# Layer norms' factors folded into their readers, and expert biases multiplied in float32, in a two-block transformer kernel

## The chip, the cores and the metric

The kernel runs on one core of a Trainium2 chip. The metric is the device time of one execution in microseconds: the median of several runs. Besides these, one execution was recorded by the hardware profiler, and all rows below come from it.

## What is computed

One sequence of 256 rows (T) of 1024 channels (D) goes through two blocks. Only the first is touched by the change:

```python
mix = token_mixer(x, w_in, b_in, sinks, ln_v_g, ln_v_b, w_spatial, b_spatial, w_out, b_out)
h = layer_norm(ALPHA * x + mix, ln1_g, ln1_b)
ffn = routed_experts(h, w_router, b_router, w_gate, b_gate, w_up, b_up, w_down, b_down)
x = layer_norm(ALPHA * h + ffn, ln2_g, ln2_b)
```

The mixer projects x by w_in into attention's q, k, v and into u and g. It runs attention in a window of 128, and beside it a spatial gate: g goes through gelu and a layer norm over groups of 64 channels (factors ln_v_g, ln_v_b), is multiplied along the sequence by a causal 128 x 128 matrix for each of 8 groups, gets b_spatial added, and is multiplied by gelu(u). Both halves together are multiplied by w_out.

The router's logits `h @ w_router + b_router` choose 4 of 32 experts for each row. An expert is `hid = min(x@w_gate+b_gate, 7)*sigmoid(...)*(clip(x@w_up+b_up)+1)`, then `hid @ w_down + b_down`, weighted by a softmax over the four logits. Each of an expert's three matrices is 1024 x 1024 in float32, 4 MiB. The second block (a recurrent mixer, attention and a feed-forward layer) follows.

## The kernel before

**Front** (`front`, lines 195 to 628). The weights of w_in and w_out arrive in pieces of 1 MB in a ring of slots. Each half piece is split into a rounded high part (a cast by ScalarE, line 1324) and a low part (a subtraction, line 1325, by VectorE or POOL as the string FRONT_LOW says); a product is then three fast matmuls (`product`). The order on each engine is the order in which the program lists the instructions; nothing is reordered. `pump` starts the next load and the next casts whenever a product has freed a slot. `after` says which small loads are put into SyncE's queue behind which piece.

POOL computes ALPHA * x at line 339 and adds b_out at line 507. VectorE and POOL normalise one block of g's 128 rows each at lines 499 to 502: subtract the mean, multiply by the inverse deviation, multiply by ln_v_g, add ln_v_b. The spatial product is evicted at lines 523 and 524. The residual then goes through `evict` (line 549, with its statistics at 551), `norm` (559, with ln1_g), `turned` (transposes, copied by ScalarE), `router` (logits, top values; lines 574 and 575) and is scaled by ScalarE (577) and shifted by ln1_b on POOL (578). `split_biases` makes three bf16 parts of b_gate and b_up on rows 0 to 95 of `bgu`, with ScalarE and POOL, between the products by w_out. `warm` issues matmuls without use that keep TensorE busy.

**Experts** (`moe`, from line 699). The chosen rows are found from the logits (lines 709 to 732; `sel` at 726). Each expert gets up to 64 rows. For every two experts `chosen` (744) makes a 0/1 matrix, and `gather` multiplies the normed rows by it, which gives the experts' inputs `xg`, transposed; VectorE (756) and ScalarE (757) evict it. For each expert `gate_up` opens two PSUM banks with the bias, then adds 16 matmuls for the gate and 16 for the up product (64 stationary columns by 512 moving ones; the two halves of the 1024 output channels use the two halves of the array's columns side by side):

```python
self.mm(p[64 * fh:64 * fh + 64, :], self.ohb[:, e:e + 1].to_broadcast([128, CAP]),
        self.bgu[:, q, fh * 512:(fh + 1) * 512], start=True, stop=False)
```

Then come swiglu on VectorE and ScalarE (801 to 806), a transpose of the hidden rows (815, 816), the down product (`y`, evicted at 823), and for two experts together the scatter (`sc`, added into the sum at 772). `start_sum`, at expert 2, writes ALPHA * h plus the weighted b_down into the sum: four matmuls on 32 rows (`sc<-bdn,gT`) and line 965. Expert 15 is finished at once, with a test for overflowing experts behind it.

The experts' weights stream through a ring of nine tiles of 2 MB (`fetch`). SyncE's queue sends for the next tile as soon as TensorE has finished with the oldest one. The first nine tiles are already loaded during the front, in slots that the front gives up one by one.

In the profile all matmuls stand under line 89 and all transposes under line 93, with the names of their tiles: `g`, `u` and `y` are the gate, up and down products, `g<-bgu,ohb` and `u<-bgu,ohb` the biases. A float32 or bf16 matmul of one column half and its neighbour of the other half run side by side.

Of the kernel before, what the change touches and what calls it, by code (L numbers as in the profile page):

```python
# [21 lines left out]
T = 256  # L22
D = 1024
# [16 lines left out]
WARM = 12, 10, 11, 20  # L40
# [31 lines left out]
class Net:  # L72
# [66 lines left out]
    def run(self):  # L139
# [16 lines left out]
        self.bgu = pb.tile([128, 2, D], BF, name="bgu")  # L156
        self.ohb = pb.tile([128, NE], BF, name="ohb")
        nc.gpsimd.memset(self.bgu[96:128], 0.0)
        nc.gpsimd.memset(self.ohb, 0.0)
# [10 lines left out]
        self.top = pb.tile([128, NT, 8], F32, name="top")  # L170
        with ExitStack() as fctx:
            self.front(fctx)
# [28 lines left out]
    def front(self, fctx):  # L201
# [41 lines left out]
        bst = fp.tile([18, 128], F32, name="bst")  # L243
        nc.scalar.dma_start(bst[0:10, :], b_in[0:1280].rearrange("(r c) -> r c", c=128))
        nc.scalar.dma_start(bst[10:18, :], a["ln1_b"].rearrange("o (r c) -> (o r) c", c=128))
# [31 lines left out]
        def after_g():  # L277
            L["bg"] = early(carve(4, 0, (512,)), bcast_rows(b_in[1280:1792], 512))
            L["lnvg"] = early(carve(4, 512, (512,)), bcast_rows(a["ln_v_g"], 512))
            L["lnvb"] = early(carve(4, 1024, (512,)), bcast_rows(a["ln_v_b"], 512))  # L280

        def after_u():
# [5 lines left out]
            L["bout"] = load("bout", [128, D], bcast_rows(a["b_out"], D))  # L288

        def after_wo():  # L290
            L["wr"] = load("wr", [128, KC, NE], a["w_router"][0].rearrange("(k p) e -> p k e", p=128))
            L["br"] = load("br", [128, NE], bcast_rows(a["b_router"], NE))
            L["ln1g"] = load("ln1g", [128, D], bcast_rows(a["ln1_g"], D))
            L["ln1b"] = load("ln1b", [128, D], bcast_rows(a["ln1_b"], D))
            bf = L["bf"] = fp.tile([128, 2 * D], F32, name="bf")
            for s in range(3):
                for q, nme in enumerate(("b_gate", "b_up")):
                    nc.sync.dma_start(bf[32 * s:32 * s + 32, q * D:(q + 1) * D], a[nme][0])

        self.pieces(spec, halves, [slot[f"r{i}"] for i in range(9)])  # L300
        self.after = {0: after_kv, 2: after_q, 4: after_g, 6: after_u, 7: after_wo}
# [13 lines left out]
        p = bank("o", [128, 18])  # L315
# [5 lines left out]
        bqs = fp.tile([128, 18], F32, name="bqs")  # L321
# [16 lines left out]
        for t in range(NT):  # L338
            G.tensor_scalar(self.h[:, t, :], self.x[:, t, :], ALPHA, None, op0=OP.mult)
# [132 lines left out]
        for i in range(3):  # L472
            scores(i)
        pg = [bank("mm", [128, 512]) for _ in range(NT)]
# [30 lines left out]
        r = self.h  # L505
        for t in range(NT):
            G.tensor_tensor(r[:, t, :], r[:, t, :], L["bout"], op=OP.add)
# [6 lines left out]
        for c0 in (0, 2):  # L514
# [8 lines left out]
            V.tensor_tensor(d, p, L["bsb"][:, c0:c0 + 2, None, :].to_broadcast([128, 2, NT, 128]), op=OP.add)  # L523
# [5 lines left out]
        wr, ln1g, ln1b = L["wr"], L["ln1g"], L["ln1b"]  # L529
        lst = [f2.tile([128, 4, 6], F32, tag="lst", name=self.nm("lst")) for _ in range(NT)]  # L530

        def by_experts(rhs, n, E):

            p = bank("s", [128, n])
            for k in range(KC):
                j = k % 4
                self.mm(p[32 * j:32 * j + 32, :], wr[:, k, :], rhs(k), start=k < 4, stop=k >= 4)
            o = f2.tile([128, n], F32, tag=f"le{n}", name=self.nm("le"))
            E(o, p)
            return o  # L540

        cb = fp.tile([128, NE], F32, name="cb")

        bf = L["bf"]
        hT = bf.rearrange("p (k t) -> p k t", k=KC)
# [6 lines left out]

        def norm(t):

            mv = f2.tile([128, 2], F32, tag="lmv", name=self.nm("lmv"))
            V.bn_aggr(mv, lst[t])
            for n in range(2):
                rr = r[:, t, n * 512:(n + 1) * 512]
                V.scalar_tensor_tensor(rr, rr, mv[:, 0:1], ln1g[:, n * 512:(n + 1) * 512],
                                       op0=OP.subtract, op1=OP.mult)  # L560
            return self.rsqrt(f2, mv[:, 1:2], 1, add=1e-5)

        def turned(t):
            for c0 in (0, 4):
                p = bank("s", [128, 4, 128])
                for c in range(4):
                    self.tr(p[:, c, :], r[:, t, (c0 + c) * 128:(c0 + c + 1) * 128])
                S.copy(hT[:, c0:c0 + 4, t * 128:(t + 1) * 128], p)

        def router(t, rs):  # L570
            le = by_experts(lambda k: hT[:, k, t * 128:(t + 1) * 128], 128, S.copy)
            p = bank("s", [128, NE])
# [1485 lines left out]
```

## Time and profile before

| | |
|---|---|
| median of 3 runs | 1548.91 us (1543.96 to 1551.39) |
| the profiled execution | 1553.83 us, of which the span from first to last instruction is 1552.2 us |
| front, to the first gate product | 0 to 124 us |
| experts, to the last down product | 124 to 1044 us |
| second block | 1044 to 1552 us |
| mean granted TensorE clock | 0.966 of 2.4 GHz |
| TensorE matmul busy | 1430.2 us, 92% of the span |
| VectorE, ScalarE, POOL busy | 613.9, 365.4, 179.3 us |
| read from HBM | 488.34 MB |

TensorE's busy time is modelled from starts and so counts some waiting as busy; whether it or the transfers bound a stage must be seen from the stage itself: from the length of a repeated stretch, and from what ended TensorE's idle time.

### The profile page before, as it was taken

What the parts mean: (1) busy time and instruction counts of PE and PEld (TensorE: products, weight loads), DVE (VectorE), ACT (ScalarE), POOL (GpSimd) and SP (SyncE); (2) the same over time, 40 slices, a digit from 0 to 9 for tenths busy, and PEclk for the clock granted to TensorE, in tenths of its full rate; (3) what the DMA queues carried; (4) which work ended last, traced back from release to release, by engine and by line L of the source; (5) the groups of instructions that cost most, each with busy time, mean ns of one, the idle gap of its engine ahead of it and who ended that gap; (6) DMA issues with size and microseconds to landing.
All of it is one profiled execution on the core that took longest, in us unless ns stands there. A gap on an engine that the chain in (4) does not pass through costs nothing. (4 is left out here: it accounts for less than half of the span.)

```text
span 1552.2 us, 19103 instructions
## 1 busy us (share of the span) xinstructions
PE 1430.2 (92%) x7944; PEld 830.2 (53%) x7944; DVE 613.9 (40%) x1087; ACT 365.4 (24%) x607; POOL 179.3 (12%) x155
## 2 busy tenths in 40 slices
PE   8789899999999989999998989897998999999998
PEld 7674333333333333333233233237877777799998
DVE  5882131222122122122124122126597547876664
ACT  4551100010110100100100110113643323365452
POOL 4630000000000011000000000004352223200000
PEclk9999989999999999999999999998988999999999
DMA  9887999999999999999999999983423124765530
GB/s 301 286 332 293 426 409 408 428 427 427 429 427 428 428 425 421 427 429 427 429 426 428 427 427 428 428 334 116 136 89 119 32 86 169 241 220 186 195 136 28
DMA packets 94510, 491.13 MB, mean 316 GB/s; under 512 B 13639, under 2 KB 44039, under 8 KB 67284
## 3 DMA queue, kind: packets, MB, share of 16 engines
q1 hardware_dynamic: 93536, 489.01, 78.2%
q8 instruction: 64, 1.05, 0.3%
q10 hardware_dynamic: 372, 0.66, 0.1%
q0 software_dynamic: 512, 0.20, 0.1%
q14 instruction: 26, 0.21, 0.0%
HBM read 488.34 MB, written 1.51 MB: 316 GB/s over the span
## 5 line engine op out<-in xcount | busy, mean ns | idle before, releaser
L89 PE MATMUL g<-w,xg 128*64 128x512 f32 x1024 | 239.0, 620 | 6.2 <-DMA w<-in_w_gate_dram 6.2
L89 PE MATMUL u<-w,xg 128*64 128x512 f32 x1024 | 227.1, 594 | 13.6 <-DMA w<-in_w_up_dram 13.6
L89 PE MATMUL y<-w,hidT 128*64 128x512 f32 x1024 | 226.9, 595 | 2.9 <-DMA w<-in_w_down_dram 1.7
L89 PEld LDWEIGHTS u<-w,xg 128*64 128x64 f32 x1024 | 70.8, 137 | 159.4 <-issue 132.6
L89 PEld LDWEIGHTS g<-w,xg 128*64 128x64 f32 x1024 | 74.5, 143 | 150.9 <-issue 137.7
L1324 ACT CAST w<-w 128x1024 fp32r<-128x1024 f32 (+1 forms) x116 | 118.7, 1035 | 148.8 <-PE pj L89 62.0
L89 PEld LDWEIGHTS y<-w,hidT 128*64 128x64 f32 x1024 | 70.8, 137 | 152.7 <-issue 144.8
L1325 POOL TENSOR_TENSOR w<-w,w 128x1024 fp32r<-128x1024 f32 (+1 forms) x33 | 79.5, 2413 | 587.8 <-ACT w L1324 582.5
L1325 DVE TENSOR_TENSOR w<-w,w 128x1024 fp32r<-128x1024 f32 x83 | 114.0, 1390 | 83.6 <-ACT w L1324 83.6
L823 ACT COPY y<-y 64x512 f32<-64x512 f32 x64 | 37.1, 579 | 369.8 <-PE y L89 369.4
L801 DVE TENSOR_SCALAR g<-g 128x512 f32<-128x512 f32 x32 | 22.1, 691 | 220.4 <-PE g L89 220.4
L816 DVE COPY hidT<-tr 128x256 f32<-128x256 f32 x32 | 13.6, 425 | 231.7 <-ACT hidT L815 231.7
L804 DVE TENSOR_SCALAR g<-u 128x512 f32<-128x512 f32 x32 | 22.1, 692 | 172.5 <-PE u L89 172.5
L89 PE MATMUL pj<-w,h2p 128*128 128x512 f32 x336 | 84.3, 408 | 0.9 <-DVE w L1325 0.9
L802 ACT ACTIVATE sg<-g 128x512 f32<-128x512 f32 x32 | 20.2, 630 | 244.9 <-DVE g L801 244.9
L89 PEld LDWEIGHTS pj<-w,h2p 128*128 128x128 f32 x336 | 64.2, 195 | 17.3 <-DVE w L1325 1.3
L89 PE MATMUL sc<-y,ogT 128*128 128x512 f32 x124 | 62.5, 619 | 3.0 <-ACT y L823 1.4
L772 DVE TENSOR_TENSOR h<-h,sc 128x512 f32<-128x512 f32 x60 | 41.1, 687 | 28.4 <-PE sc L89 28.4
L1325 DVE TENSOR_TENSOR wp<-w,wp 128x1024 fp32r<-128x1024 f32 x32 | 38.4, 1224 | 18.6 <-ACT wp L1324 18.6
L89 PE MATMUL mm<-w,xp 128*128 128x512 f32 (+1 forms) x168 | 37.3, 383 | 6.3 <-DVE xp L329 6.3
L1065 POOL MEMSET late_scratch<- 128x128 f32 x1 | 0.2, 205 | 366.8 <-PEq L899 366.8
L89 PEld LDWEIGHTS tr<-oh,x 128*128 128x128 f32 x256 | 32.0, 203 | 17.9 <-issue 17.9
(537 smaller groups left out, 1858.9 us busy)
## 6 DMA issues: line engine op xcount, KB each, us to landing
w<-in_w_up_dram SPq DMA_DIRECT2D x58, 2048.0 KB, 32.2
w<-in_w_down_dram SPq DMA_DIRECT2D x58, 2048.0 KB, 33.8
w<-in_w_gate_dram SPq DMA_DIRECT2D x56, 2048.0 KB, 33.9
w<-in_w_in_dram SPq DMA_DIRECT2D x27, 1024.0 KB, 5.2
w<-in_w_ffn_up_dram SPq DMA_DIRECT2D x22, 1024.0 KB, 5.2
w<-in_w_gate_dram SPq DMA_DIRECT2D x16, 1024.0 KB, 11.6
w<-in_w_up_dram SPq DMA_DIRECT2D x12, 1024.0 KB, 7.3
w<-in_w_down_dram SPq DMA_DIRECT2D x12, 1024.0 KB, 13.9
```

Source lines behind the costliest of these rows:

```text
L89: return self.nc.tensor.matmul(out, lhsT, rhs, start=start, stop=stop)
L772: nc.vector.tensor_tensor(dst, dst, pp[dh], op=OP.add)
L801: nc.vector.tensor_scalar(g1, pg, 7.0, None, op0=OP.min)
L802: nc.scalar.activation(sg, g1, AF.Sigmoid, scale=1.702)
L804: nc.vector.tensor_scalar(g1, pu, -7.0, 7.0, op0=OP.max, op1=OP.min)
L816: nc.vector.tensor_copy(hidT[:, 2:4].rearrange("p j f s -> p j (f s)"), p[:, 2:4])
L823: nc.scalar.copy(yv[64 * i:64 * i + 64, hf * 512:(hf + 1) * 512], py[64 * hf:64 * hf + 64, :])
L1065: nc.gpsimd.memset(self.vstage[0], 0.0)
L1324: nc.scalar.copy(t[:, 0], src)
L1325: self.low[j % len(self.low)].tensor_tensor(t[:, 1], src, t[:, 0].bitcast(F32), op=OP.subtract)
```

## The change

- **Loads.** ln_v_g, ln_v_b, ln1_g and ln1_b are no longer broadcast to 128 rows. They come as short rows that are transposed into columns (`bst`, 34 rows instead of 18) by four loads on ScalarE's queue instead of one, and ln1's once more in the gather's order (`norm1`, two loads). b_spatial and b_out are loaded earlier. b_gate and b_up are loaded once, in float32, to rows 0 to 63.
- **Residual.** ALPHA * x + b_out is made by VectorE, after the attention's scores, instead of by POOL in two steps.
- **Spatial gate.** g is normalised without factors, the first block by VectorE (two operations), the second by ScalarE (eight). ln_v_g multiplies at the eviction of the spatial product; ln_v_b times the spatial matrices' row sums (eight matmuls after the scores) is added to b_spatial.
- **Router.** It reads the residual itself, transposed before its mean and deviation are known; its weights are multiplied by ln1_g, and the mean is taken off the logits by the weights' column sums. Transposes and router products stand between the last products by w_out (`between`).
- **Scaling.** ScalarE writes the normed rows with mean and deviation, without factors (`spread`). The gather's eviction multiplies by ln1_g and adds ln1_b (`normed`), in four instructions of 128 columns instead of two of 256. `start_sum` multiplies by ln1_g, broadcast by two loads from POOL's queue, and takes ln1_b as a 33rd row of its matmul.
- **Experts' biases.** `split_biases` is gone. A bias is a float32 matmul on 32 rows.
- **Warming.** 14 instead of 20 matmuls before the routing, and 4 within it.

```diff
-WARM = 12, 10, 11, 20
+WARM = 12, 10, 11, 14, 4
-        self.bgu = pb.tile([128, 2, D], BF, name="bgu")
-        self.ohb = pb.tile([128, NE], BF, name="ohb")
+        self.bgu = pb.tile([64, D], F32, name="bgu")
...
-        for t in range(NT):
-            G.tensor_scalar(self.h[:, t, :], self.x[:, t, :], ALPHA, None, op0=OP.mult)
...
+                V.scalar_tensor_tensor(r[:, t, ns], self.x[:, t, ns], ALPHA, L["bout"][:, ns], op0=OP.mult, op1=OP.add)
+
+        p = bank("s", [128, 4, 128])
+        for gg in range(8):
+            self.mm(p[64 * (gg % 2):64 * (gg % 2) + 64, gg // 2, :], self.ones[:, 0:64], wT[:, gg, :])
+        for c in range(4):
+            V.scalar_tensor_tensor(L["bsb"][:, c], p[:, c], bqs[:, 30 + c:31 + c], L["bsb"][:, c], op0=OP.mult, op1=OP.add)
...
-        for t, E in ((0, V), (1, G)):
-            gt, js = g[:, 8 * t:8 * t + 8], slice(8 * t, 8 * t + 8)
-            E.tensor_tensor(gt, gt, mv[:, js, 0:1].to_broadcast([128, 8, 64]), op=OP.subtract)
-            E.tensor_tensor(gt, gt, rs[:, js, None].to_broadcast([128, 8, 64]), op=OP.mult)
-            E.tensor_tensor(gx[:, t], gx[:, t], L["lnvg"], op=OP.mult)
-            E.tensor_tensor(gx[:, t], gx[:, t], L["lnvb"], op=OP.add)
+        nb = fp.tile([128, 8], F32, name="gnb")
+        V.scalar_tensor_tensor(nb, mv[:, 8:16, 0], -1.0, rs[:, 8:16], op0=OP.mult, op1=OP.mult)
+        for j in range(8):
+            S.activation(g[:, 8 + j, :], g[:, 8 + j, :], AF.Identity, scale=rs[:, 8 + j:9 + j], bias=nb[:, j:j + 1])
+        gt = g[:, 0:8]
+        V.tensor_tensor(gt, gt, mv[:, 0:8, 0:1].to_broadcast([128, 8, 64]), op=OP.subtract)
+        V.tensor_tensor(gt, gt, rs[:, 0:8, None].to_broadcast([128, 8, 64]), op=OP.mult)
...
-            G.tensor_tensor(r[:, t, :], r[:, t, :], L["bout"], op=OP.add)
...
         for t in range(NT):
             evict(t, 0, po[t])
-        next(biases, None)
+        cc = fp.tile([128, 2], F32, name="cc")
+        V.tensor_copy(cc[:, 0:1], by_experts("b", wr, lambda k: bqs[:, 10 + k:11 + k], 1))
+        V.tensor_copy(cc[:, 1:2], by_experts("m", wrg, lambda k: self.ones[:, 0:1], 1))
...
-            if i == 1:
-                pc = bank("s", [128, NE])
-                self.mm(pc, c4.to_broadcast([128, 128]), ist)
-                V.tensor_tensor(cb, pc, L["br"], op=OP.add)
+            if i == 0:
+                pc = bank("s", [128, 2, NE])
+                for x in range(2):
+                    self.mm(pc[:, x, :], cc[:, x:x + 1].to_broadcast([128, 128]), ist)
...
+            elif i > 1:
+                turned(i - 2, 0, 4)
         evict(0, 1, p)
         fac[0] = norm(0)
+        between = {(0, 0): lambda: routed(0, 0, 4), (0, 1): lambda: turned(0, 4, 4), (0, 2): lambda: routed(1, 0, 4),
+                   (0, 3): lambda: routed(0, 4, 4), (256, 0): lambda: logits(0), (256, 1): lambda: router(0),
+                   (256, 2): lambda: turned(1, 4, 2), (256, 3): lambda: routed(1, 4, 2)}
...
+            if q:
+                turned(1, 6, 2)
+                routed(1, 6, 2)
+                logits(1)
+                spread(0)
+                fac[1] = norm(1)
+                router(1)
+                spread(1)
...
+        def normed(o, p, c, dve):
+
+            g, b = (self.norm1[:, i, c:c + 1] for i in range(2))
+            if dve:
+                nc.vector.tensor_scalar(o, p, g, b, op0=OP.mult, op1=OP.add)
+            else:
+                nc.scalar.activation(o, p, AF.Identity, scale=g, bias=b)
...
-                nc.vector.tensor_copy(xg[b][:, c0:c0 + 2, :], p[:, 0:2])
-                nc.scalar.copy(xg[b][:, c0 + 2:c0 + 4, :], p[:, 2:4])
+                for c in range(4):
+                    normed(xg[b][:, c0 + c, :], p[:, c, :], c0 + c, c < 2)
...
-                    self.mm(p[64 * fh:64 * fh + 64, :], self.ohb[:, e:e + 1].to_broadcast([128, CAP]),
-                            self.bgu[:, q, fh * 512:(fh + 1) * 512], start=True, stop=False)
+                    r = slice(32 * q, 32 * q + 32)
+                    self.mm(p[64 * fh:64 * fh + 64, :], self.ident[r, 32 * q + e:32 * q + e + 1].to_broadcast([32, CAP]),
+                            self.bgu[r, fh * 512:(fh + 1) * 512], start=True, stop=False)
...
-            for t in range(NT):
-                for n in range(2):
+            lng = [m2.tile([128, 512], F32, tag=tag, bufs=1, name=self.nm("lng")) for tag in ("g1", "sg")]
+            for n in range(2):
+                nc.gpsimd.dma_start(lng[n], bcast_rows(a["ln1_g"][:, n * 512:(n + 1) * 512], 512))
+            for n in range(2):
+                cs = slice(n * 512, (n + 1) * 512)
+                for t in range(NT):
                     p = bank("sc", 2, [128, 512])
...
+                    r = self.acc[:, t, cs]
+                    nc.vector.tensor_tensor(self.by_rows(r), self.by_chunks(self.h[:, t, cs]), self.by_rows(lng[n]),
+                                            op=OP.mult)
+                    nc.vector.scalar_tensor_tensor(r, r, ALPHA, p, op0=OP.mult, op1=OP.add)
```

## Rows read from the trace of the kernel before

**Rows 1.** The page's second part: the transfers' busy tenths in 40 slices.
```profile
DMA  9887999999999999999999999983423124765530
```

**Rows 2.** Stretches: us; busy of PE, PEld, DVE, ACT, POOL; clock; DMA share, GB/s.
```profile
233.65:257.09 23.44, 23.44 (x106) 7.63 (x105) 3.14 (x4) 1.47 (x3) 0.00 (x0) 0.93 0.96 396
289.12:344.60 55.48, 53.40 (x253) 19.98 (x252) 11.40 (x18) 5.44 (x11) 0.00 (x0) 0.97 1.01 428
344.60:398.37 53.77, 51.70 (x252) 19.58 (x251) 11.40 (x18) 5.44 (x11) 0.00 (x0) 1.00 1.01 427
...
507.62:629.28 121.66, 108.46 (x502) 42.05 (x502) 22.59 (x36) 10.88 (x22) 11.23 (x40) 0.96 1.01 425
629.28:979.58 350.30, 320.02 (x1504) 117.96 (x1504) 77.74 (x162) 33.15 (x68) 0.00 (x0) 0.99 1.01 427
861.30:920.11 58.81, 52.80 (x251) 19.36 (x251) 11.39 (x18) 5.44 (x11) 0.00 (x0) 1.00 1.01 427
979.58:1021.00 41.42, 37.12 (x173) 11.73 (x172) 4.96 (x7) 3.16 (x6) 0.00 (x0) 1.00 1.01 428
```

**Rows 3.** TensorE's groups: busy us, mean ns, then idle time before them and releasers.
```profile
L89 PE MATMUL g<-w,xg 128*64 128x512 f32 x1024 | 239.0, 620 | 6.2 <-DMA w<-in_w_gate_dram 6.2
L89 PE MATMUL u<-w,xg 128*64 128x512 f32 x1024 | 227.1, 594 | 13.6 <-DMA w<-in_w_up_dram 13.6
L89 PE MATMUL y<-w,hidT 128*64 128x512 f32 x1024 | 226.9, 595 | 2.9 <-DMA w<-in_w_down_dram 1.7 <-ACT hidT L815 1.1
```

**Rows 4.** Timeline, expert 0: start, us, engine, operation, tiles, count [idle before].
```profile
124.43 7.03 PE L89 MATMUL g<-w,xg 128*64 128x512 f32 x32
...
131.30 0.38 PE L89 MATMUL u<-bgu,ohb 128*64 128x512 bf16 x2
131.51 1.02 PE L89 MATMUL u<-w,xg 128*64 128x512 f32 x4
```

**Rows 5.** Timeline, the start of the sum at expert 2.
```profile
192.65 6.26 PE L89 MATMUL sc<-bdn,gT 32*128 32x512 f32 x8 [0.45 <-ACT gT L959]
...
195.53 1.02 DVE L965 SCALAR_TENSOR_TENSOR h<-x,sc 128x512 f32<-128x512 f32 x1 [0.68 <-PE sc L89]
```

**Rows 6.** Stretches, within that start of the sum.
```profile
194.35:196.05 1.70, 1.70 (x3) 0.61 (x2) 1.02 (x2) 0.00 (x0) 0.00 (x0) 0.50 1.02 434
```

**Rows 7.** Timeline, the end of a down product.
```profile
182.64 7.03 PE L89 MATMUL y<-w,hidT 128*64 128x512 f32 x32
...
189.61 0.66 PE L93 MATMUL tr<-ident,hid 128*128 128x128 f32 x4
```

**Rows 8.** Timeline, the second half of a gather and the scatter behind it.
```profile
219.78 0.42 DVE L756 COPY xg<-sc 128x256 f32<-128x256 f32 x1 [1.36 <-PE sc L89]
...
220.66 0.30 PEld L89 LDWEIGHTS sc<-y,ogT 128*128 128x128 f32 x2 [0.89 <-ACT xg L757]
```

**Rows 9.** Timeline of the front, ahead of the product by w_out.
```profile
67.36 1.66 DVE L501 TENSOR_TENSOR w<-w,w 128x512 f32<-128x512 f32 x1
...
70.11 6.08 POOL L507 TENSOR_TENSOR h<-h,bout 128x1024 f32<-128x1024 f32 x2
70.62 7.80 DVE L1325 TENSOR_TENSOR w<-w,w 128x1024 fp32r<-128x1024 f32 x3
...
79.08 7.80 PE L89 MATMUL mm<-w,xp 128*128 128x512 f32 x22 [6.26 <-DVE xp L329]
85.67 1.23 DVE L1325 TENSOR_TENSOR w<-w,w 128x1024 fp32r<-128x1024 f32 x1 [0.47 <-ACT w L1324]
```

**Rows 10.** Timeline of the front, behind w_out's first half.
```profile
92.88 0.31 PE L89 MATMUL s<-bqs,wr 128*32 128x1 f32 x16
...
105.80 0.42 DVE L549 TENSOR_TENSOR h<-h,mm 128x256 f32<-128x256 f32 x1
...
115.07 2.78 DVE L726 TENSOR_TENSOR sel<-rgt,req 128x64 bf16<-128x64 f32 x1
...
119.08 1.19 PE L89 MATMUL tr<-oh,x 128*128 128x128 f32 x4 [0.94 <-DVE oh L744]
```

More of the change, by code (lines that the diff above doesn't have):

```diff
@@ L292, in after_wo @@
             L["br"] = load("br", [128, NE], bcast_rows(a["b_router"], NE))
[L293 to L298, printed above, removed]
+            for q, nme in enumerate(("b_gate", "b_up")):
+                nc.sync.dma_start(self.bgu[32 * q:32 * q + 32, :], a[nme][0])
         self.pieces(spec, halves, [slot[f"r{i}"] for i in range(9)])
-        self.after = {0: after_kv, 2: after_q, 4: after_g, 6: after_u, 7: after_wo}
+        self.after = {0: after_kv, 2: after_q, 4: after_g, 7: after_wo}
         self.pump()
@@ L522, in front @@
             uv = uT[:, c0:c0 + 2, :]
-            V.tensor_tensor(d, p, L["bsb"][:, c0:c0 + 2, None, :].to_broadcast([128, 2, NT, 128]), op=OP.add)
+            for c in range(2):
+                V.scalar_tensor_tensor(d[:, c], p[:, c], bqs[:, 26 + c0 + c:27 + c0 + c],
+                                       L["bsb"][:, c0 + c, None, :].to_broadcast([128, NT, 128]), op0=OP.mult, op1=OP.add)
             V.tensor_tensor(uv, uv, d.rearrange("p c t s -> p c (t s)"), op=OP.mult)
@@ L551, in evict, with turned, routed @@
                 V.bn_stats(lst[t][:, 2 * n + (q + x) // 256, :], rr[:, x:x + 256])
+        def turned(t, c0, n):
+            p = bank("s", [128, n, 128])
+            for c in range(n):
+                self.tr(p[:, c, :], r[:, t, (c0 + c) * 128:(c0 + c + 1) * 128])
+            S.copy(hT[:, c0:c0 + n, t * 128:(t + 1) * 128], p)
+        def routed(t, c0, n):
+            by_experts(t, wrg, lambda k: hT[:, k, t * 128:(t + 1) * 128], 128, range(c0, c0 + n))
+            if c0 + n == KC:
+                le[t] = f2.tile([128, 128], F32, tag="le", name=self.nm("le"))
+                S.copy(le[t], pe[t])
@@ L561, in norm @@
[L561 to L572, printed above, removed]
-            self.mm(p, le, ist)
-            V.scalar_tensor_tensor(self.lg[:, t, :], p, rs, cb, op0=OP.mult, op1=OP.add)
+            V.tensor_scalar(nm[:, 0:1], mv[:, 0:1], -1.0, None, op0=OP.mult)
@@ L575, in router @@
+            return self.rsqrt(f2, mv[:, 1:2], 1, add=1e-5), nm
+        def router(t):
+            p, (rs, nm) = pl[t], fac[t]
+            q = f2.tile([128, NE], F32, tag="lq", name=self.nm("lq"))
+            V.scalar_tensor_tensor(q, cb[:, 1], nm[:, 0:1], p, op0=OP.mult, op1=OP.add)
+            V.scalar_tensor_tensor(self.lg[:, t, :], q, rs, cb[:, 0], op0=OP.mult, op1=OP.add)
             V.max(self.top[:, t, :], self.lg[:, t, :])
-            S.activation(self.by_chunks(self.x[:, t, :]), self.by_rows(r[:, t, :]), AF.Copy, scale=rs)
@@ L578, in router, with spread @@
-            G.tensor_tensor(self.by_chunks(self.x[:, t, :]), self.by_chunks(self.x[:, t, :]), self.by_rows(ln1b), op=OP.add)
-        biases = self.split_biases(bf[0:96].rearrange("p (q c) -> p q c", q=2))
+            V.tensor_tensor(nm[:, 1:2], nm[:, 0:1], rs, op=OP.mult)
+        def spread(t):
+            rs, nm = fac[t]
+            S.activation(self.by_chunks(self.x[:, t, :]), self.by_rows(r[:, t, :]), AF.Identity, scale=rs, bias=nm[:, 1:2])
         def out_half(p, ts, i, w, cs=slice(0, 512)):
@@ L614, in front @@
                     freed()
-                    if i == 1:
-                        turned(0)
+                between.get((q, i), lambda: None)()
             evict(1, 1, p, q, 256)
-        fac[1] = norm(1)
-        router(0, fac[0])
-        turned(1)
-        router(1, fac[1])
+            if q:
[6 more added lines that the diff above has]
+                spread(1)
         self.warm(bank("o", [128, 128]), self.ident, WARM[3])
@@ L918, in overflow @@
                             self.mm(p[:, k, :], self.h[:, t, k * 128:(k + 1) * 128], oh[:, t], start=t == 0, stop=t == NT - 1)
-                    nc.vector.tensor_copy(xo, p)
+                    for k in range(KC):
+                        normed(xo[:, k, :], p[:, k, :], k, True)
                     def weights(nme):
```

98 lines of the change are left out of this document (44 added, 54 removed).

## The prediction

> **What bounds the kernel now.** I read the page's slices first, then TensorE's own stretches, then single instructions. The DMA engines are busy nine tenths or more from slice 5 to slice 26 [rows 1], which says "bound by the weights' transfers". The expert stage shows that this is only its second half. I cut the stage where the gate bias of each even expert begins, so that one stretch is two experts. From expert 4 to expert 14 there are five such stretches, 55.47, 55.48, 53.77, 55.47 and 53.78 us, mean 54.79; one of either length stands in [rows 2]. In none of them does TensorE wait for a weight: that is TensorE's own pace. Two experts' weights are 25.2 MB, 58.8 us at the 428 GB/s shown, and the late stretch of 58.81 us [rows 2] is just that. So in the first half TensorE runs ahead of the transfers, eating up the ring of nine 2 MB tiles that was full at the start (18.9 MB, 44 us of transfer), and loses some lead at expert 15 (121.66 us for four experts [rows 2] where the pace would take 109.6). Only from expert 18 on does it wait: 350.30 us for twelve experts against 6 x 54.79 = 328.7, and 41.42 us from expert 30's gate bias to the end of expert 31's up product [rows 2] against 37.6 at its own pace (23.44 from expert 4's gate bias to expert 5's [rows 2], and two products of 7.1). TensorE therefore waits for weights 21.6 + 3.8 = 25.4 us in all; the idle times put down to weights, 6.2 + 13.6 + 1.7 us [rows 3], sum to 21.5. **That, 21.5 to 25.4 us, is all the room there is for TensorE work that is added in the experts**; beyond it each microsecond is on the path. After the experts nothing is changed.
>
> **Experts' biases.** Before, a bias is two bf16 matmuls on 128 rows (the float32 value split into three bf16 parts), one per half of the columns, side by side: the up product's begins at 131.30 and the product itself at 131.51, 0.21 us [rows 4]. After, it is two float32 matmuls on 32 rows. What does a float32 one cost? A product of 16 float32 matmuls of the same 64 x 512 output takes 6.87 us from its start to the next bias (124.43 to 131.30) [rows 4], 0.86 us for each such pair. Fewer rows don't shorten it: the four float32 matmuls of b_down on 32 rows follow each other by 1.70 us (VectorE takes the second's result for 1.02 us after waiting 0.68) [rows 5] at a granted clock of 0.50, 1.2 GHz [rows 6], which is 0.85 at full clock, for 512 columns by a full stationary of 128. That is four passes of 512 columns. So a bias pair goes from 0.21 to 0.85, +0.64 us, twice an expert: 64 x 0.64 = **+41.0 us** on TensorE. Nothing on TensorE hides it, since it works in order.
> The Trainium skill, "Perfetto Trace Analysis", Engine Utilization, gives float32 in its low-high form half the output rate, not a quarter; by that a pair would cost 0.43 us and the term would be an estimated 14 us. The trace of b_down speaks against it.
>
> **Switching between 32 and 128 rows.** Bias to product, product to bias and bias to product again is three changes of the array's rows per expert that weren't there. The trace has no such change between 64-column matmuls. Nearest are a product followed by a transpose (128 x 64 to 128 x 128): the product of 182.64 should end after 6.86 us, at 189.50, and the transposes begin at 189.61 [rows 7], 0.1 us; and b_down's end, where no gap is seen. I take the middle, 0.05 x 96 = **+4.8 us**, with 0 to 15 us for the range. The skill's "TensorEngine Tiling (Array Packing)", Key Properties, says that changing the tiling mode drains the engine; it would make the upper end likelier, and only runs can tell.
>
> **Gather.** Each quarter-row eviction (VectorE 0.42 us, then ScalarE) becomes two with a factor and a shift. The scatter's second matmul waits for ScalarE's part (0.89 us idle at 220.66) [rows 8]; two short instructions in place of one on either engine add an estimated 0.15 us each, so 0.3 us in each of 15 gathers: **+4.5 us** (0 to 6).
>
> **Start of the sum.** ln1's factor is now put on the residual here: four more VectorE operations of 1.02 us (the strided form's price [rows 5]) beside four of some 0.7, 7.0 us against 4.1. But TensorE's matmuls set the pace there, 1.70 us each, and the first operation needn't wait for them. The factor's two broadcasts are sent from POOL's queue into swiglu's tiles once expert 2's swiglu is done, a whole down product (some 7 us) ahead of use; late, they hold VectorE, and TensorE behind its two banks. **+1 us** (0 to 5).
>
> **Front.** It ends where the first gate product starts, and every microsecond there moves the whole stage. Step by step:
> - Ahead of the w_out product TensorE idles 6.26 us until 79.08, for a VectorE queue in which three low-part casts take 7.80 us while POOL adds b_out (6.08 us); alone one takes 1.23 [rows 9]: 4.1 us go. So do two products by ln_v's factors (one of 1.66 us [rows 9]): 3.3 more. Against that VectorE makes the residual and the spatial shift after the scores, some 4 us, of which 3 fall into its wait for ScalarE. And ScalarE gets the eight normalisations ahead of three casts and the gelus, which hold back the attention product. I let the product start 3 us earlier, not 7.
> - From the end of w_out's first half (92.88) to the last product, whose eviction begins at 105.80 [rows 10]: the router's constants are now copied after both evictions (4 of some 0.7 us, behind a cast of 1.23) where TensorE needs them one product later: a new wait of some 3.5 us; the transposes and router matmuls moved in here are 2.3 more. +5.8.
> - From 105.80 to the gather at 119.08 [rows 10]: 13.3 us. The second block's turning, router and scaling are mostly gone from it, and with POOL's add the collision that made `sel` 2.78 us instead of 0.2 [rows 10]. I count the chain left (eviction, statistics, rsqrt, logits, routing) at 7.1: -6.2.
> - The gather's first four matmuls take 1.19 us [rows 10], over twice what 128 columns take at full clock; continuous matmuls ahead of it should save an estimated 1 us.
> - Two MB less of broadcasts and casts there free no engine that ends last; the new loads on ACT's queue are issued before its first work at 7 us.
> Sum -3 + 5.8 - 6.2 - 1 = -4.4, say **-5 us** (-9 to -1).
>
> **The sum.** 41.0 + 4.8 + 4.5 + 1 - 5 = +46.3 on TensorE's line, of which 25.4 fill its waits: **+20.9 us**. Is the transfers' line later? TensorE's pace becomes 54.8 + 2.6 + 0.3 + 0.3 = 58.0 a pair, still under 58.8, and the ring, full at expert 4 and filled again at expert 15, loses under 1 us a pair: it never runs dry, so the waits vanish wholly. The profiled execution took 1553.8 us, so it becomes 1574.7; the median of the runs shown is 4.9 lower, 1548.9, which gives **1570 us**, slower.
>
> **The rivals.**
> 1. *The float32 bias is half as dear* (0.43 a pair). Then TensorE's line gains 64 x (0.43 - 0.21) + 4.5 + 1 - 5 = 14.6 us, less than 21.5, the transfers stay the bound and the end moves with the front, -5, plus what the transfers idle more in the first experts (0.3 x 5 + 1): 1546 us, not slower. The point that decides is 0.8 us of added TensorE work per expert (25.4 / 32). Its mechanism is two passes over the columns instead of four. Against it: the spacing of b_down's matmuls [rows 5, 6]. Chance 0.11. (This is the case that the skill's page on trace analysis, cited above, would give.)
> 2. *The transfers' line stays last all the same*: the pace of experts 4 to 14 is not kept, or biases overlap with the product behind them. The end then moves by -5 plus the idle time of transfers whose slots come late, 5 x 1.5 us before expert 5 and some 5 at expert 15: +7, 1556 us. For it: the two lines lie within 13 us. Chance 0.09.
> 3. *The clock falls more often.* In three of the five stretches the clock's mean is 0.97 and they are 1.7 us longer [rows 2]: it falls after TensorE's wait for the gates. If a slow bias behind that wait made it fall in every pair, 14 x 0.7 = 10 us, with switches at 0.1 us, 5 more: 1585 us. Chance 0.12.
> 4. *The front gains nothing* (its new waits eat all): 1575, within the forecast.
>
> **How the numbers follow.** Forecast 0.68, with 1560 to 1580 as its own range. Leaving out rival 1 and the upper part of rival 3 leaves out 0.18: 1552 to 1584. Slower by over 0.5% (7.7 us, about what a measurement of this kernel can tell from no change): the forecast, rival 3 and a small part of rival 2, 0.82. Same: most of rivals 1 and 2, 0.14. Faster: rival 1 with a front gain at its upper end, 0.04.
>
> **What would show it.** Right: stretches of two experts of 57.5 to 59 us from the start; no wait of TensorE for weights in late experts; 0.85 us between a bias and its product; the DMA share under 1.0 in more stretches; the gather beginning some 4 us earlier. Wrong: bias pairs of 0.2 to 0.45 us, late stretches at 58.8 with waits for weights, or a first gate product more than 12 us earlier.

## The result, and the profile after

The changed kernel takes **1594.94 us** (median of four runs, 1593.93 to 1599.51) beside 1550.04 of the kernel before: ratio 1.0303, 95% interval 1.0268 to 1.0338, slower by 45 us where +21 was forecast. The profiled execution took 1599.51 us with a span of 1597.9 us, against 1552.2 before: 45.7 us.

The transfers' slices, which stood at 9 from slice 5 to 26 [rows 1], change little, and mislead again:

```profile
DMA  9769989999999999999999999981433124665540
```

The stretches answer to [rows 2] (us; busy of PE, PEld, DVE, ACT, POOL; clock; DMA share, GB/s): an early and a late pair of experts, experts 14 to 17, 18 to 29, and the last two.

```profile
300.47:361.64 61.17, 58.37 (x260) 20.64 (x259) 12.01 (x20) 6.31 (x13) 0.00 (x0) 0.95 0.98 411
545.64:669.36 123.72, 114.32 (x517) 40.86 (x516) 23.78 (x40) 12.62 (x26) 11.00 (x40) 0.97 0.98 407
669.36:1028.03 358.67, 339.88 (x1551) 121.84 (x1550) 81.38 (x174) 38.39 (x80) 0.00 (x0) 0.98 0.99 419
912.01:970.02 58.01, 55.21 (x259) 19.99 (x258) 12.01 (x20) 6.31 (x13) 0.00 (x0) 1.00 1.01 427
1028.03:1067.60 39.57, 39.57 (x182) 12.34 (x181) 4.96 (x7) 3.16 (x6) 0.00 (x0) 1.00 0.94 392
```

Early pairs take 61.17 us where they took 53.77 to 55.48, and the DMA share is under 1.0 in four of these five rows. In TensorE's groups (busy us, mean ns, then idle time and releasers) the waits for weights of [rows 3] are gone, and VectorE's addition now holds up the scatter (the last line is the scatter's group before the change):

```profile
L89 PE MATMUL g<-w,xg 128*64 128x512 f32 x1024 | 251.4, 648 | 0.0
...
L89 PE MATMUL u<-w,xg 128*64 128x512 f32 x1024 | 226.8, 595 | 0.0
...
L89 PE MATMUL sc<-y,ogT 128*128 128x512 f32 x124 | 62.5, 619 | 11.7 <-DVE h L793 10.3
```

```profile
L89 PE MATMUL sc<-y,ogT 128*128 128x512 f32 x124 | 62.5, 619 | 3.0 <-ACT y L823 1.4 <-DVE h L772 1.0
```

TensorE no longer waits for weights anywhere in the experts: it is last throughout, as forecast. How long one bias takes is seen in expert 0's timeline (start, us, engine, operation, tiles, count), as in [rows 4]:

```profile
117.93 1.07 PE L89 MATMUL g<-bgu,ident 32*64 32x512 f32 x4
118.93 7.09 PE L89 MATMUL g<-w,xg 128*64 128x512 f32 x32
125.95 1.07 PE L89 MATMUL u<-bgu,ident 32*64 32x512 f32 x4
126.95 1.51 PE L89 MATMUL u<-w,xg 128*64 128x512 f32 x6
```

Bias to product is 1.00 us (0.21 before) and product to next bias 7.02 us (6.87 before), so from gate bias to up bias 8.02 us instead of 7.11: 0.91 us a bias, of which four passes explain 0.64. That 8.02 is the clean interval, though. Behind TensorE's wait for the gates it is much longer; the timeline of expert 6 and, under it, the stretch of the same interval and of one without a fall:

```profile
299.99 0.55 PE L93 MATMUL tr<-ident,og 128*128 128x128 f32 x2 [2.02 <-DVE og L814]
300.47 1.97 PE L89 MATMUL g<-bgu,ident 32*64 32x512 f32 x4
302.37 9.34 PE L89 MATMUL g<-w,xg 128*64 128x512 f32 x32
311.64 1.07 PE L89 MATMUL u<-bgu,ident 32*64 32x512 f32 x4
```

```profile
300.47:311.64 11.17, 11.17 (x37) 3.04 (x36) 0.00 (x0) 0.37 (x1) 0.00 (x0) 0.71 0.85 333
854.00:862.02 8.02, 8.02 (x37) 2.41 (x36) 0.00 (x0) 0.37 (x1) 0.00 (x0) 1.00 1.00 423
```

The granted clock averages 0.71 there: it lies at 1.2 GHz for part of the interval and at 2.4 GHz for the rest. Taken over all 32 experts, the intervals exceed the clean one by 34.3 us after the change and by 23.9 us before it; but 6.2 us of the 23.9 are waits for the gate's weights [rows 3], all in these intervals, so 17.7 us at most belong to the clock. The twelve that are over 1 us too long after the change all come before expert 22.

The gather's evictions (VectorE 0.42 us [rows 8] and ScalarE 0.37 before) and the scatter behind them:

```profile
285.74 0.73 DVE L765 TENSOR_SCALAR xg<-sc,norm 128x128 f32<-128x128 f32 x2 [1.06 <-PE sc L89]
286.84 0.81 ACT L767 ACTIVATE xg<-sc,norm 128x128 f32<-128x128 f32 x2 [1.25 <-PE sc L89]
287.34 3.03 PE L89 MATMUL sc<-y,ogT 128*128 128x512 f32 x6 [0.78 <-DVE h L793]
```

From up bias to the next gate bias an expert with a gather and a scatter takes 26.5 us where it took 24.93, and one without takes 15.47 where it took 14.63. So the bias is 0.84 us of the 1.57, and the gather costs 0.73 us. There are twelve such experts.

One stretch became shorter. From expert 15's up bias to the next gate bias, in which the test for overflowing experts stands, it is 46.22 us before and 40.20 after, although the bias grew; the line above the stretches is TensorE's longest wait in it before, for which the trace shows no cause:

```profile
577.81 2.08 PE L89 MATMUL tr<-oh,x 128*128 128x128 f32 x8 [2.63 <-issue]
```

```profile
538.16:584.38 46.22, 36.94 (x156) 15.85 (x152) 10.40 (x17) 4.06 (x8) 8.13 (x21) 0.93 1.01 426
```

```profile
580.50:620.70 40.20, 34.72 (x156) 13.71 (x154) 11.00 (x19) 4.85 (x10) 4.72 (x11) 1.00 1.01 427
```

The start of the sum ([rows 5] before) is held by VectorE, and the front's TensorE rows answer to [rows 9, 10]:

```profile
193.36 2.86 PE L89 MATMUL sc<-bdn,gT 33*128 33x512 f32 x4 [0.45 <-ACT gT L984]
...
196.95 3.81 PE L89 MATMUL sc<-bdn,gT 33*128 33x512 f32 x4 [0.73 <-DVE h L996]
```

```profile
76.84 11.29 PE L89 MATMUL mm<-w,xp 128*128 128x512 f32 x48
88.06 0.30 PE L89 MATMUL s<-bqs,wr 128*32 128x1 f32 x16
...
93.34 0.63 PE L89 MATMUL s<-ist,cc 128*128 128x32 f32 x4 [3.27 <-DVE cc L615]
...
107.27 0.42 DVE L558 TENSOR_TENSOR h<-h,mm 128x256 f32<-128x256 f32 x1 [1.60 <-PE mm L89]
...
112.50 0.23 DVE L738 TENSOR_TENSOR sel<-rgt,req 128x64 bf16<-128x64 f32 x1
...
114.19 2.02 PE L89 MATMUL tr<-oh,x 128*128 128x128 f32 x16
```

The first gate bias comes at 117.93 instead of 124.19. From there to the end of expert 31's up product (1021.00 before, 1067.57 after) the stage grew by 52.8 us; behind that the two traces take the same time within 1 us.

### The profile page after: what moved, and what is told of

Its sections match the earlier page's. It is cut to its first block, busy times and chain, and to the rows that moved or that the text cites. A ratio compares the mean times of both kernels' runs of the same rounds, so it can differ in the third digit from the quotient of the medians.

```text
span 1597.9 us, 19498 instructions
## 1 busy us (share of the span) xinstructions
PE 1491.1 (93%) x8102; PEld 832.1 (52%) x8102; DVE 612.0 (38%) x1138; ACT 374.6 (23%) x644; POOL 143.8 (9%) x140
## 5 line engine op out<-in xcount | busy, mean ns | idle before, releaser
L89 PE MATMUL g<-w,xg 128*64 128x512 f32 x1024 | 251.4, 648 | 0.0
L1356 DVE TENSOR_TENSOR w<-w,w 128x1024 fp32r<-128x1024 f32 x83 | 106.8, 1302 | 85.6 <-ACT w L1355 85.5
L89 PE MATMUL sc<-y,ogT 128*128 128x512 f32 x124 | 62.5, 619 | 11.7 <-DVE h L793 10.3
L767 ACT ACTIVATE xg<-tr,norm 128x128 f32<-128x128 f32 x32 | 12.9, 454 | 138.3 <-DVE xg L765 136.4
L89 PEld LDWEIGHTS sc<-y,ogT 128*128 128x128 f32 x124 | 20.0, 189 | 45.6 <-DVE h L793 32.8
L89 PE MATMUL g<-bgu,ident 32*64 32x512 f32 x128 | 42.1, 739 | 0.0
## 6 DMA issues: line engine op xcount, KB each, us to landing
w<-in_w_down_dram SPq DMA_DIRECT2D x58, 2048.0 KB, 13.8
```

The lines of the kernel that those rows point to most:

```text
L89: return self.nc.tensor.matmul(out, lhsT, rhs, start=start, stop=stop)
L767: nc.scalar.activation(o, p, AF.Identity, scale=g, bias=b)
L1356: self.low[j % len(self.low)].tensor_tensor(t[:, 1], src, t[:, 0].bitcast(F32), op=OP.subtract)
```

## The experiments

Theory A: the loss is TensorE's, made of the biases' passes, of changes of the array's rows around them and of falls of the clock. The rivals of each run are in its expectation. Ratios are to the kernel before, with 95% intervals, and kernels are compared by them. "Interval" is gate bias to up bias; "excess" is the sum over 32 experts of what the intervals have above the kernel's shortest.

**The biases alone, in the kernel before.**

```diff
-                    self.mm(p[...], self.ohb[:, e:e + 1].to_broadcast([128, CAP]), self.bgu[:, q, ...], ...)
+                    r = slice(32 * q, 32 * q + 32)
+                    self.mm(p[...], self.ident[r, 32 * q + e:32 * q + e + 1].to_broadcast([32, CAP]), self.bgu[r, ...], ...)
-        biases = self.split_biases(...)
```

> The kernel before with the float32 biases alone, without their splitting. Theory A: 64 x 0.91 = 58 us more of TensorE work, 21.5 to 25.4 of it in its waits for weights, and 0 to 10 for more falls of the clock: 1582 to 1594 us, no wait for weights left, gate to up 8.02 us where the clock is full. Rival (half of the loss comes from the other parts, the gather and the start of the sum): 1565 to 1578 us. If the clock falls of the changed kernel come from the longer gather ahead of the gates and not from the biases, gate intervals stay at 8.8 plus 0.9 us in a few pairs; if from the slow 32-row biases, 11 us in most pairs as there.

Measured: 1599.75 us, ratio 1.0300 (1.0281 to 1.0320), 5.8 us beyond theory A's range. No wait for weights is left, the clean interval is 8.02 us, the excess 39.2 us. This one part alone is as slow as the whole change, whose dearer gather and earlier front nearly cancel; the rival falls. Two slow intervals of its trace:

```profile
301.19:312.39 11.20, 11.20 (x37) 3.03 (x36) 0.00 (x0) 0.37 (x1) 0.00 (x0) 0.71 0.92 357
361.67:371.33 9.66, 9.66 (x37) 2.73 (x36) 0.00 (x0) 0.37 (x1) 0.00 (x0) 0.82 1.01 410
```

They nearly alternate, with the short gather of before: the deep falls come with the 32-row biases, not with the longer gather. The first gate bias is at 124.00 us: in the old front, leaving out the biases' splitting gains 0.2 us.

**The biases alone put back, in the changed kernel.**

```diff
-        self.bgu = pb.tile([64, D], F32, name="bgu")
+        self.bgu = pb.tile([128, 2, D], BF, name="bgu")
+            if i != 1:
+                next(biases, None)
+    def split_biases(self, bf):
...
+        nc.gpsimd.tensor_tensor(bf, bf, bgu[0:96], op=OP.subtract)
...
+        nc.gpsimd.tensor_tensor(bf[64:96], bf[64:96], bgu[64:96], op=OP.subtract)
```

> The changed kernel with the biases alone put back: three bf16 parts on 128 rows, their casts and subtractions by ScalarE and POOL, the transposed residual again in the biases' tile. Theory A (biases made TensorE the bound of the whole stage): gate to up 7.11 us again, pairs of experts 55.5 to 57.5 us early, waits for weights of 10 to 25 us in the late experts again, and the time set by the transfers and the earlier front: 1540 to 1553 us. Rival 1 (the gather's factors, the gates' wait with its clock falls and the start of the sum are worth 15 us and more by themselves): 1558 to 1575 us. Rival 2 (the front's gain hangs on the biases' casts being gone): the first gate product begins at 123 to 126 us instead of 118, and the time is 1550 to 1556.

Measured: 1555.13 us, ratio 1.0020 (1.0010 to 1.0030). The interval is 7.11 us again, early pairs take 54.5, and waits for weights are back (2.4 + 12.7 us): the transfers are last again, so rival 1 falls. But the first gate bias comes at 126.70 us, 2.5 us later than before the change and 0.7 later than rival 2 said; the time is rival 2's (1550 to 1556), 2 us beyond theory A's. The timelines of POOL, VectorE, ScalarE and TensorE show why; under them the changed kernel's last cast:

```profile
83.59 4.12 POOL L679 TENSOR_TENSOR bf<-bf,bgu 96x2048 f32<-96x2048 f32 x1 [25.27 <-issue]
...
84.44 5.49 DVE L1384 TENSOR_TENSOR w<-w,w 128x1024 fp32r<-128x1024 f32 x2 [1.52 <-ACT w L1383]
...
87.74 1.90 ACT L681 CAST bgu<-bf 32x2048 bf16<-32x2048 f32 x1 [1.91 <-POOL bf L679]
...
91.69 4.05 POOL L683 TENSOR_TENSOR bf<-bf,bgu 32x2048 f32<-32x2048 f32 x1 [3.98 <-ACT bgu L682]
...
92.65 4.17 DVE L1384 TENSOR_TENSOR w<-w,w 128x1024 fp32r<-128x1024 f32 x1 [2.72 <-ACT w L1383]
...
99.69 1.06 PE L89 MATMUL s<-ist,cc 128*128 128x32 f32 x4 [10.26 <-DVE cc L624]
```

```profile
89.25 1.23 DVE L1356 TENSOR_TENSOR w<-w,w 128x1024 fp32r<-128x1024 f32 x1 [1.51 <-ACT w L1355]
```

While POOL subtracts (4.12 us, and 4.05 later) VectorE's casts (line 1384) take 5.49 us for two and 4.17 for one, where each of the changed kernel's takes 1.23. The last one also starts 3.4 us later (92.65 against 89.25), since ScalarE's cast ahead of it stands behind copies of the biases that wait for POOL. The router's constants, queued behind it, hold TensorE for 10.26 us instead of 3.27: some 2.9 us are the stretched cast and 3.4 the later start. The Trainium skill, "SBUF — State Buffer", SBUF: two separate sides, says that the pair of ports that VectorE and GpSimd (POOL) share is held by one of them for a whole instruction while the other is blocked. The rows agree: the cast that began at 92.65 ended at 96.82, 1.1 us after POOL's subtraction did.

**The biases on all rows.** Same float32 matmuls, 128 rows of which 64 are zero: the array keeps its rows.

```diff
-                    self.mm(p[...], self.ident[r, 32 * q + e:32 * q + e + 1].to_broadcast([32, CAP]), self.bgu[r, ...], ...)
+                    self.mm(p[...], self.ident[:, 32 * q + e:32 * q + e + 1].to_broadcast([128, CAP]), self.bgu[:, ...], ...)
```

> The changed kernel, its biases' two float32 matmuls on all 128 rows (64 of them zero) where they have 32; two passes over nothing else change. The changed kernel's trace has 0.91 us more per bias than the kernel before: from bias to product 1.00 us where it was 0.21 (prediction: 0.85 from four passes of 512 columns), and some 0.12 us more between a product's end and the next bias. Theory A (the part above 0.64 is the change of the array's rows, 32 to 128 and back, 0.27 us a bias): bias to product 0.85 us, gate to up 7.75 us instead of 8.02, 64 x 0.27 = 17 us less: 1578 us (1574 to 1583). Rival (the part above 0.64 belongs to float32 weight loads or to the matmuls themselves, not to the rows): no change, 1592 to 1598 us. Where the granted clock falls after the wait for the gates: under both about as often as in the changed kernel.

Measured: 1568.60 us, ratio 1.0103 (1.0083 to 1.0122). TensorE's timeline:

```profile
289.77 1.08 PE L89 MATMUL g<-bgu,ident 128*64 128x512 f32 x4
290.68 7.04 PE L89 MATMUL g<-w,xg 128*64 128x512 f32 x32
297.54 1.03 PE L89 MATMUL u<-bgu,ident 128*64 128x512 f32 x4
298.40 1.03 PE L89 MATMUL u<-w,xg 128*64 128x512 f32 x4
```

Bias to product is 0.86 us at the up product and the interval 7.77, 0.25 us less, close to theory A's 0.27; from up bias to the next gate bias it is 15.28 instead of 15.47, 0.19 less. That makes 32 x 0.44 = 14.1 us for the rows. The part that stays, 7.77 - 7.11 = 0.66, is the four passes. That the change of rows costs this, and not a matmul on 32 rows by itself, follows from b_down, whose 32-row matmuls come 1.70 us apart at half clock [rows 5, 6], which is 0.85 at full clock, no slower than the 0.86 of 128-row ones. Neither range held the time, since the expectation left the falls as they were: the excess fell from 34.3 to 17.1 us, about 1.7 us in each fall, although the wait for the gates in front is still 2.02 us.

**Matmuls in the wait for the gates.**

```diff
             if b:
+                self.warm(bank("u", 2, [128, 128]), self.ident, 8)
                 list(gates_of(b))
```

> The changed kernel with eight float32 matmuls of 128x128 (some 1.7 us, results unused) put ahead of the gates' transposes, in TensorE's wait of 2.0 us for VectorE's product of the gates, in every pair of experts but the first. In the changed kernel the gate interval behind that wait is 11.0 to 11.4 us at a granted clock of 0.71 in nine pairs, where 8.02 is the clean one: 34.3 us above 8.02 over all experts. Theory A (the clock falls because TensorE stands in that wait): with it covered nearly all gate intervals are 8.02 to 8.1 us and the time falls by 25 to 34 us, to 1561 to 1570 us, as long as the transfers (some 1545 to 1550) stay ahead. Rival 1 (the clock falls for what the gather's narrow matmuls and the 32-row biases do, wait or not): intervals stay near 11 us, time 1590 to 1610. Rival 2 (the transfers are the bound by then): 1580 to 1590 with new waits for weights.

Measured: 1571.50 us, ratio 1.0127 (1.0104 to 1.0150). The excess is 6.6 us instead of 34.3, with three falls left (experts 1, 3 and 21, each with other waits of TensorE in or ahead of it, which the added matmuls don't cover), and the span 29.5 us shorter. Expert 6's timeline:

```profile
291.68 1.95 PE L89 MATMUL u<-ident 128*128 128x128 f32 x16
293.87 0.41 PE L93 MATMUL tr<-ident,og 128*128 128x128 f32 x2 [0.24 <-DVE og L814]
294.21 1.07 PE L89 MATMUL g<-bgu,ident 32*64 32x512 f32 x4
295.21 7.09 PE L89 MATMUL g<-w,xg 128*64 128x512 f32 x32
302.23 1.07 PE L89 MATMUL u<-bgu,ident 32*64 32x512 f32 x4
```

The gates' transposes come 2.19 us after the added matmuls began, so nothing is lost, the interval is 8.02, and the clock stays at 2.4 GHz. Theory A holds, 1.5 us beyond its range: the falls come from TensorE standing still for 2 us.

**Both mends.** The two diffs together.

> Both mends of the changed kernel at once: biases' float32 matmuls on 128 rows, and eight matmuls ahead of the gates' transposes. Singly they gave 1568.6 and 1571.5 us beside 1552.6 of the kernel before and some 1599 of the changed one. Theory A (a TensorE line of 64 x 0.25 us of row changes and some 28 to 34 us of slow gate intervals, which add up until the transfers are last): e1 has 17.1 us left in slow gate intervals, e4 has 64 x 0.25 = 16 us left in row changes, so 1552 to 1557 us, gate to up 7.78 us nearly everywhere, and first waits for weights. Rival (what the two mend is one and the same, since e1 halved the slow intervals too): 1562 to 1569 us.

Measured: 1556.03 us, ratio 1.0033 (1.0014 to 1.0052). A pair and the gate product's group:

```profile
347.69:404.81 57.12, 56.10 (x275) 22.38 (x274) 12.00 (x20) 6.31 (x13) 0.00 (x0) 1.00 1.01 428
```

```profile
L89 PE MATMUL g<-w,xg 128*64 128x512 f32 x1024 | 227.5, 597 | 0.0
```

The time is theory A's; its waits for weights are not there, and TensorE is still last. Against the changed kernel the ratios give 42 us: 14.1 of row changes and 28.1 of excess (34.3 to 6.2). So row changes and falls are two causes. But the gains of the two mends, 31 and 27 us singly, don't add up, since 32 rows also deepen the falls that the added matmuls prevent.

**The gather without its factors**, beside the mend of the clock. This kernel leaves ln1's factor and shift out of what the experts get, so it computes something else; only its time is of use.

```diff
-                for c in range(4):
-                    normed(xg[b][:, c0 + c, :], p[:, c, :], c0 + c, c < 2)
+                nc.vector.tensor_copy(xg[b][:, c0:c0 + 2, :], p[:, 0:2])
+                nc.scalar.copy(xg[b][:, c0 + 2:c0 + 4, :], p[:, 2:4])
```

> As e4 (eight matmuls ahead of the gates' transposes), and the gather's evictions are plain copies of two quarters each, as in the kernel before: ln1's factor and shift are left out of what the experts get. Against e4. Theory A (TensorE's line is last, so the gather's longer evictions count in full; up to next gate is 26.49 us in e4 and 24.93 + 0.91 = 25.84 without them): 14 to 15 gathers of 0.65 us, 9 to 10 us less than e4, 1561 to 1564 us. Rival 1 (the other transfers or a later wait take it back): within 3 us of e4. Rival 2 (the prediction's 0.3 us was right and the rest lies elsewhere): 4 to 5 us less.

Measured: 1563.87 us, ratio 1.0092 (1.0058 to 1.0125), in theory A's range. Against the mend alone that is 0.35% less by the ratios, 5.4 us, nearer to rival 2. Up bias to next gate is 25.77 us instead of 26.50 in the twelve experts with a gather and a scatter between, 0.73 us each, 8.8 us; the first gate bias came 1.9 us later in this execution. By the times alone rival 2 isn't shut out, since the two intervals overlap; by the spacing it is. TensorE's group shows where the 0.73 us lay, in the scatter's wait for VectorE's addition, 1.0 us in all instead of 10.3:

```profile
L89 PE MATMUL sc<-y,ogT 128*128 128x512 f32 x124 | 62.5, 619 | 3.1 <-ACT y L844 1.4 <-DVE h L793 1.0
```

**Biases in two bf16 parts, without POOL.** A value is kept as the sum of two bf16 numbers, where the kernel before keeps three.

```diff
-        self.bgu = pb.tile([64, D], F32, name="bgu")
+        self.bgu = pb.tile([128, D], BF, name="bgu")
+        self.ohb = pb.tile([128, 64], BF, name="ohb")
+        nc.gpsimd.tensor_tensor(self.ohb, self.ident[:, 0:64], self.ident[:, 64:128], op=OP.add)
...
+        S.copy(self.bgu, L["bf"])
...
+                V.tensor_tensor(self.bgu[64:128], L["bf"][64:128], self.bgu[64:128], op=OP.subtract)
...
+                    self.mm(p[...], self.ohb[:, 32 * q + e:32 * q + e + 1].to_broadcast([128, CAP]), self.bgu[:, ...], ...)
```

> The changed kernel with biases in two bf16 parts on 128 rows, split in the front by one ScalarE cast and one VectorE subtraction, none of it on POOL. In e2 POOL's two subtractions of 4.1 us stretched three of VectorE's casts from 1.23 to 2.7 and 4.2 us, and the first gate product came at 126.7 instead of 118 us. Theory A (the front's gain hangs on POOL being still, and the time of a kernel bound by its transfers follows the front): first gate product at 117 to 120 us, gate to up 7.11, 10 to 25 us of waits for weights again, and 1544 to 1549 us beside 1552.6, faster than both. Rival 1 (the weights' transfers don't start earlier with the front): 1550 to 1555, with more waits for weights. Rival 2 (TensorE still last because of the gather's 0.65 us a pair and clock falls): 1553 to 1560 without waits for weights.

Measured: **1542.58 us, ratio 0.9945 (0.9925 to 0.9964)**, faster than both kernels. First gate bias at 118.25 us, interval 7.11; VectorE's subtraction, an early pair and TensorE's groups:

```profile
93.03 1.22 DVE L632 TENSOR_TENSOR bgu<-hT,bgu 64x1024 bf16<-64x1024 f32 x1
```

```profile
340.84:395.34 54.50, 51.70 (x251) 19.60 (x251) 12.00 (x20) 6.31 (x13) 0.00 (x0) 1.00 1.01 432
```

```profile
L89 PE MATMUL g<-w,xg 128*64 128x512 f32 x1024 | 237.1, 617 | 2.0 <-DMA w<-in_w_gate_dram 2.0
L89 PE MATMUL u<-w,xg 128*64 128x512 f32 x1024 | 226.6, 593 | 10.8 <-DMA w<-in_w_up_dram 10.8
```

The subtraction lies in a stretch in which VectorE has nothing else to do; theory A holds. With the transfers last the time follows the front: first gate bias at 118.25, 124.19 and 126.70 us went with 1542.6, some 1551 and 1555.1.

**The same, with matmuls in the wait for the gates.**

> e10 with the eight matmuls ahead of the gates' transposes. Theory A (the transfers are last, slow gate intervals are hidden in waits for weights): the same as e10 within 3 us; slow intervals gone, waits for weights longer by about as much. Rival (slow intervals delay the slots and so the transfers, or TensorE is last in part): 4 to 15 us less than e10.

Measured: 1539.63 us, ratio 0.9940 (0.9919 to 0.9961). The excess fell from 16.8 to 11.9 us and the waits for weights rose from 12.8 to 15.6: theory A. The 95% intervals overlap nearly whole, so the 3 us aren't shown to be a gain over the run before it.

## Why the prediction was right in direction and wrong in size

By its own steps, with what the trace or a run gave, in us of TensorE's line:

| step | forecast | measured | from |
|---|---|---|---|
| biases, four passes | +41.0 | +42.2 | 64 x 0.66, biases on all rows |
| changes of rows | +4.8 | +14.1 | 32 x 0.44, the same run |
| gather | +4.5 | +8.8 | 12 x 0.73 |
| start of the sum | +1 | +1.1 | expert 2, less its bias |
| front | -5 | -6.3 | 117.93 against 124.19 |
| falls of the clock | 0 | +16.6 | 34.3 against 17.7 |
| waits for weights filled | -25.4 | -21.5 | idle times of [rows 3]; none left |
| the test at expert 15 | 0 | -5.4 | 40.20 against 46.22, less 0.84 of bias and 1.5 of waits counted above |
| put down to no step | | -3.0 | what is left |
| end of the experts | +20.9 | +46.6 | 1067.57 against 1021.00 |

In what is left are slow starts behind the waits for weights: a late pair's wait of 2.26 us before the change came with 2.7 us (27.64 instead of 24.93 from up bias to next gate bias). The forecast's 25.4 had them in, since it was taken from the lengths of stretches.

**Right.** The float32 bias is four passes, not two: a pair costs 0.66 us more, and rival 1 falls. The half rate that the Trainium skill, "Perfetto Trace Analysis", Engine Utilization, states for the low-high form of float32 would make that an estimated 0.43 - 0.21 = 0.22; these float32 matmuls don't run at it. All waits for weights vanish (rival 2 falls), and the rest of the program doesn't move. Putting the biases back brought the waits for weights back. That the clean pair takes 58.01 us, as the forecast's 58.0, is partly luck: the forecast added 3.2 us to a pace of 54.8 that holds 1.0 us of falls, while the clean pair grew by 4.24, from 53.77.

**Wrong: "Switching between 32 and 128 rows", 0.05 x 96.** An expert has four such changes, not three (the one into the gate's bias was left out), and one takes 0.44 / 4 = 0.11 us, not 0.05. Of the two places chosen as nearest, the product with its transposes [rows 7] changes the columns of a stationary while all 128 rows stay in use, and doesn't price a change of rows. b_down's end does change the rows, but the ends of matmuls are modelled, so that no gap seen there says nothing. What was measured, 14.1 us, lies just under the upper end that the forecast gave for this term, 15 us. The rule of the Trainium skill, "TensorEngine Tiling (Array Packing)", Key Properties, that a change of tiling mode drains the engine, had been given as the reason for that end; the 0.25 and 0.19 us that the run with 128-row biases saved agree with it.

**Wrong: the clock was costed at nothing.** This is the largest miss, 16.6 us. Rival 3 named the mechanism and the place (TensorE's wait for the gates, a slow bias behind it) and a price of 10 us, and had it at 0.12; the sum had no term for it. It expected more falls, and there were some more: up to expert 15 nine intervals are over 1 us too long instead of six, from there on three as before (four more that were too long before hold a wait for weights of 1.1 to 1.6 us). But chiefly the falls became deeper, which neither the sum nor the rival had: nine of the twelve are 3.0 to 3.4 us long, with 32-row biases behind the wait, where 1.7 to 2.2 is the size up to expert 15 before. [rows 2] already showed pairs 1.7 us longer at a clock of 0.97, in a stretch where TensorE sets the pace; the forecast took them into its pace and asked no further in the sum.

**Wrong: "Gather", 0.3 us each.** Estimated as two more short instructions; the evictions grew by 0.31 us on VectorE (0.73 against 0.42) and 0.44 on ScalarE (0.81 against 0.37 us for line 757's copy before), 0.75 where 0.3 was estimated, and 0.73 reached TensorE, in the twelve gathers with a scatter behind them and not in 15. It came there through the wait for VectorE's addition of the scatter's first result (0.78 us), not through the wait for ScalarE's eviction that the forecast reckoned with. The upper bound of 0 to 6 us was too low as well.

**Not foreseen: the test at expert 15.** The stretch lost 5.4 us that no step of the forecast has, and made the miss smaller. Before, TensorE stood for 2.63 us at 577.81 between the gather's transposes and ran at a mean clock of 0.93; after, neither is seen (1.00). No run shows why.

**The front** came out near the forecast by partly other steps, so partly by luck: w_out's product starts 2.2 us earlier (3 forecast), its first half takes 11.2 us instead of 13.8 (not forecast), the stretch to the last eviction 6.3 more (5.8; the new wait is 3.27 where 3.5 was said), from there to the gather 6.4 less (6.2), and to the first bias 1.4 less (1). What the prediction missed is in the words that the smaller broadcasts and casts "free no engine that ends last": in the old order of the front that is so (the biases alone gained 0.2 us), in the new order POOL's subtractions, with the copies that wait for them, would have cost 126.70 - 117.93 = 8.8 us.

Without its falls of the clock the changed kernel took 1571.5 us, close to the 1570 forecast, but for reasons that cancel: an excess of 6.6 us instead of 17.7 and the gain at expert 15 on one side, dearer row changes and a dearer gather on the other.

## What to carry to other kernels

A change that looks like less work (no bf16 parts, no splitting) can move work onto the engine that is nearly last: count passes per operand type, and count every change of the array's rows, with a price measured on a change of rows. When one engine runs just ahead of the transfers, a busy DMA share says little; the idle time that the engine has left for weights is the whole budget, and it is spent once. A wait of 2 us on TensorE costs more than 2 us where the clock falls behind it, and a few matmuls without use in that wait can be worth 1.8% (1.0303 against 1.0127) where TensorE is last, and nothing that could be measured here where the transfers are.

## What the runs showed of the hardware

- A change of the stationary's rows between 32 and 128 costs TensorE about 0.11 us: a bias on 32 rows instead of 128 adds 0.25 us to the gate's interval (8.02 against 7.77) and 0.19 us behind the up bias (15.47 against 15.28), two changes each.
- A 2.02 us wait in front of 32-row float32 biases is followed by an interval of 11.17 us at a mean clock of 0.71; in front of the same matmuls on 128 rows by 9.47 us or 7.77 (no fall); with 1.95 us of matmuls in it by 8.02 us at full clock. Why the falls are deeper with 32 rows stays open: no run varied the rows apart from the time that the changes take. The wait alone isn't enough, either: from expert 22 on the changed kernel has the same 2.02 us wait in every pair, and no fall behind it (8.02 us). Why stays open too.
- POOL's subtraction of 4.1 us on float32 stretched a 1.23 us cast of VectorE to 4.17 us.
